# A decoder layer on one core: the sum of gated branches kept in DRAM by accumulating DMAs, its SBUF room given to a sixth weight slot and two high-part buffers

## Chip, cores and metric

One core of a Trainium2 chip runs the kernel. The metric is the device time of one execution in microseconds (us); a shorter one is better.

## The reference, cut

The kernel computes one layer for 256 tokens of width 2048: a norm, one wide input product, four attention branches, their gated sum and an output product. All numbers are float32.

```python
h = rms_norm(x, norm_w)
p = h @ w_in                                  # (256, 2048) @ (2048, 17492)
(z, gate, dsa_qkv, idx_q, idx_k, idx_w, fox_qkv, fox_f, diff_qkv, dil_qkv) = jnp.split(p, IN_OFFSETS, axis=-1)
# o_dsa: top-64 of indexer scores, then attention; o_fox: forgetting; o_diff: difference of two
# softmax maps; o_dil: dilated windows.  Four heads of 128 each.
for b in range(4):
    y = branches[b].reshape(bsz, seq, 512) * jax.nn.silu(z_parts[b])
    term = jax.nn.sigmoid(g_parts[b]) * (y @ w_branch[b])      # (256, 2048)
    merged = term if merged is None else merged + term
x = x + merged @ w_out
return rms_norm(x, final_norm_w)
```

## The kernel before

**Tiles and units.** The weights are read once, in blocks of 512 rows by 512 columns (1 MB). A *unit* (`Unit`) is one use of one such block. Its matmuls run in float32r, so each block is split: ScalarE copies it rounded, the *high part* (`whi`, L192), and VectorE subtracts that from the block, the *low part* (`wlo`, L193), each in two halves of 1024 columns. `three` (L342) then issues three matmuls for one product: high by high (L345), high weight by low activation (L346), low weight by high activation (L347).

**Slots and buffers.** A block is loaded by SP's queue into one of five *slots* (`raw0` to `raw4`, 8 KB of a partition each). `free` issues the next load of a slot when the split of its block is done (L195 to L198); the load itself waits until every reader of the old block is done. High and low parts have six buffers each (`HALVES`). In the main loop (L1148) the half that is split stands five halves ahead of the half whose matmuls are issued (L1153), so each engine's queue holds splits, evictions and attention steps in one fixed order.

**Seven products.** `seven` (L415) computes a 256 by 1024 block of a product in 11 units. For half of the rows of the weights it uses seven products instead of eight of a two by two scheme: the weight blocks B11, B12, B21, B22 stand in slots 0, 1, 3, 2 and are added in place on VectorE (`plus`, L171) between uses, and the activations' combinations are in `sf` (`act_forms`). The other half is done plainly by c2a, c2b, c1a and c1b, 24 matmuls each, all four in slot 4 (L448). The order is P5 P1 P3 c2a P6 c2b P7 P2 c1a P4 c1b. What a unit wants done first (`pre`, in-place sums) is issued two units ahead, right after the split of a unit's second half (L1141).

**Order of the program.** Indexer units; then for each of four branches a seven-product for q and k, one for z and v, two for the gates (`gate_units`), and four projections of 24 matmuls (`branch_units`). Attention steps are generators (`active`) that `run_threads` advances by one step for each 20 matmuls or more; a unit's `need` runs the named ones to their end first. The gate tiles g (four buffers, shared with q, k, z) hold sigmoids. After a projection VectorE multiplies it by g (L904) and adds it to m (L905), a 16 KB tile of a partition. In the last branch `merge_thread` transposes m into mT, and `act_forms` makes sf from its first half; then comes the product with w_out, one seven-product and two blocks of plain units. `open_final` loads x and the final norm's weights again (L918, L920) on POOL's queue, 3 MB.

Of the kernel before, what the change touches and what calls it, by code (L numbers as in the profile page):

```python
# [31 lines left out]
HALVES = 6  # L32
PACE = 20
SLOTS = 5
# [46 lines left out]
class Unit:  # L81
# [3 lines left out]

    def __init__(self, raw, mm, post=(), need=(), start=(), pre=(), frees=None, loads=None):
        self.raw, self.k0, self.nk, self.n = raw, raw.k0, raw.nk, raw.n
        self.mm, self.post = mm, list(post)
        self.need, self.start, self.pre = list(need), list(start), list(pre)
        self.after = []  # L90
        self.frees = [raw] if frees is None else list(frees)
        self.loads = [raw] if loads is None else list(loads)
        self.parts = [None, None]
        self.cost = 24
# [7 lines left out]
    def part(self, k, i):  # L102
        half = self.nk // 2
        return self.parts[k // half][i][:, k % half * self.n:(k % half + 1) * self.n]
# [3 lines left out]
def body(ctx: ExitStack, tc, x, norm_w, w_in, fox_b_f, lq1, lk1, lq2, lk2, subln_w,  # L108
# [70 lines left out]
    def split(u, h, hi=None, lo=None, parts=1, part=None):  # L179

        n_ = u.nk // 2 * u.n
        if not part:
            if hi is None:
                hi = wp.tile([P, 1024], F32R, name="whi", tag="whi", bufs=HALVES)
                lo = wp.tile([P, 1024], F32R, name="wlo", tag="wlo", bufs=HALVES)
            u.parts[h] = (hi[:, :n_], lo[:, :n_])
        hi, lo = u.parts[h]
        raw = u.raw.tile[:, h * n_:(h + 1) * n_]
        step = n_ // parts
        for i in range(parts) if part is None else (part,):  # L190
            s_ = slice(i * step, (i + 1) * step)
            nc.scalar.activation(hi[:, s_], raw[:, s_], AF.Copy)  # L192
            nc.vector.tensor_tensor(lo[:, s_], raw[:, s_], hi[:, s_].bitcast(F32),  # L193
                                    op=ALU.subtract)
        if h == 1:  # L195
            for f in u.after:
                f()
            free(u.frees)  # L198

# [34 lines left out]
    xs = big.tile([P, 2, D], F32, name="xs", tag="m")  # L234
# [162 lines left out]
    def act_forms(T, pool, tag):  # L397

        V["sf"] = big.tile([P, 2, 8, 2, P], F32R, name="sf", tag="sf")
        a = pool.tile([P, 2, 8, P], F32, name="asum", tag=tag)  # L400
        for t in range(2):
            c = T[:, 0:8, :, t * P:(t + 1) * P].bitcast(F32)
            nc.vector.tensor_tensor(a[:, t], c[:, :, 0], c[:, :, 1], op=ALU.add)
        yield
        a11, a12, a21, a22 = a[:, 0, 0:4], a[:, 0, 4:8], a[:, 1, 0:4], a[:, 1, 4:8]
# [4 lines left out]
        for t in range(2):  # L410
            nc.scalar.activation(V["sf"][:, t, :, 0], a[:, t], AF.Copy)
            nc.vector.tensor_tensor(V["sf"][:, t, :, 1], a[:, t],
                                    V["sf"][:, t, :, 0].bitcast(F32), op=ALU.subtract)

    def seven(src, c1, c2, base, ev, name, need=((), (), (), ()), start=()):  # L415

        st = {}
        B11, B12 = Raw(0, src, 0, 4, c1, 512), Raw(1, src, 0, 4, c2, 512)
        B21, B22 = Raw(3, src, 4, 4, c1, 512), Raw(2, src, 4, 4, c2, 512)

        def whole(half, k0):
            t = slice(half * P, (half + 1) * P)
            return lambda k: (base()[:, k0 + k, 0, t], base()[:, k0 + k, 1, t])

# [3 lines left out]
        def product(bank, act, first=False):  # L428
            def mm(u, h):
                if first and h == 0:  # L430
                    st[bank] = main_ps(name)
# [25 lines left out]
        u5 = Unit(B12, product("W", form(1, 4), True), loads=[B12, B11, B22, B21], frees=[],  # L457
                  post=[read(ev.p5, "W")], need=need[0])
        u1 = Unit(B11, product("Y", whole(0, 0), True), loads=[], frees=[],
                  post=[read(ev.p1, "Y")])  # L460
        u3 = Unit(B22, product("Z", form(0, 4), True), loads=[], frees=[])
        c2a = c(8, c2, "ZW")
        c2a.need += need[1]
        u6 = Unit(B12, product("Y", form(0, 0)), loads=[], frees=[], post=[read(ev.u2, "Y")])
        c2b = c(12, c2, "ZW")
        c2b.need += need[2]
        c2b.post += [read(ev.c12, "Z", True)]
        u7 = Unit(B11, product("Y", form(1, 0)), loads=[], post=[read(ev.u3, "Y")])
        u2 = Unit(B21, product("X", whole(0, 4), True), loads=[], frees=[],
                  post=[read(ev.c22, "W", True)])  # L470
        c1a = c(8, c1, "XY")
        u4 = Unit(B21, product("Y", whole(1, 4)), loads=[])
        u4.pre += [lambda: plus(B21, B12), lambda: free([B12])]
        c1b = c(12, c1, "XY")
        c1b.post += [read(ev.c11, "X", True), read(ev.c21, "Y", True), ev.end]
        c1b.start += start
        c1b.need += need[3]
        u5.pre += [lambda: plus(B12, B11)]
        u6.pre += [lambda: plus(B12, B22), lambda: free([B22])]
        u7.pre += [lambda: plus(B11, B12, ALU.subtract)]  # L480
        for u in (u1, u5, u3, u6, u7, u2, u4):
            u.cost = 12
        return [u5, u1, u3, c2a, u6, c2b, u7, u2, c1a, u4, c1b]

    class Tok:


        def __init__(self, dst, s1, s2, end):
            self.dst, self.s1, self.s2, self.end = dst, s1, s2, end
# [51 lines left out]
    def qkvz_units(b, off, scale, start):  # L541


        def two(names):
            if b == 0:
                if "tok" not in V:
                    V["tok"] = big.tile([P, 4, 2, 512], F32, name="tok", tag="m")
                return V["tok"][:, names == "zv"], V["tok"][:, 2 + (names == "zv")]
            return [big.tile([P, 2, 512], F32, name="tok", tag="g", bufs=4) for _ in range(2)]

        def dst_qk():
            V["q_"], V["k_"] = d = two("qk")
            return d
# [636 lines left out]
```

## Time and profile before

| | |
|---|---|
| median of two runs | 1085.38 us (1085.06 to 1085.7) |
| profiled execution, its own time | 1085.43 us |
| its span, first to last instruction | 1083.7 us |
| TensorE matmuls busy | 979.7 us (90%), 4443 |
| VectorE busy | 867.1 us (80%), 1035 instructions |
| ScalarE busy | 622.9 us (57%) |
| granted TensorE clock, mean | 0.969 of full speed |
| DMA | 187.42 MB, mean 173 GB/s |

The profile is one execution. Busy time is that of each engine's own instructions; matmuls overlap, so their durations are longer than their distance. "Idle before" is the time an engine stood still ahead of an instruction, and what follows the arrow is the instruction or transfer that ended it. The chain of waits follows the last instruction back through what released each step.

### The profile page before, as it was taken

The page shows a single profiled execution, that of the slowest core. Times are in us where ns is not written, and L with a number is a line of the kernel's source. Part 1 is how long each engine was busy: PE and PEld are TensorE (multiplying, and loading weights), DVE is VectorE, ACT ScalarE, POOL GpSimd, SP SyncE. Part 2 cuts the span into 40 slices and gives each one's busy share as a digit, 9 for nine tenths or more (in the row PEclk, how much of TensorE's full clock was granted, in tenths as well). Part 3 has the DMA queues.
Part 4 walks back from the last instruction along what each step waited for, and adds up shares of the span by engine and source line. Part 5 has one row for each costly group of instructions (what it writes and reads, how often), then busy time and mean ns, then how long its engine had stood idle before and what let it go on. Part 6 is the DMA issues. An engine that isn't in the chain of part 4 may idle for free.

```text
span 1083.7 us, 12059 instructions
## 1 busy us (share of the span) xinstructions
PE 979.7 (90%) x4443; PEld 793.9 (73%) x4443; DVE 867.1 (80%) x1035; ACT 622.9 (57%) x809; POOL 31.7 (3%) x51
## 2 busy tenths in 40 slices
PE   9989996888999999899899997869999979876997
PEld 8867884676788787777788775658888858654886
DVE  5799989778689988777899876869988968588663
ACT  5665764676546565855465657554465676534551
POOL 2010000000000000000000000000000000000010
PEclk9989997999999999999999999989999999987999
DMA  9836451535646465365266451562646534742542
GB/s 322 254 101 201 151 195 53 180 117 194 217 153 228 161 224 167 121 229 191 97 233 219 169 191 42 184 207 95 233 155 232 176 136 156 268 158 78 195 155 78
DMA packets 97739, 187.42 MB, mean 173 GB/s; under 512 B 7555, under 2 KB 9765, under 8 KB 97296
## 3 DMA queue, kind: packets, MB, share of 16 engines
q1 hardware_dynamic: 96240, 181.06, 49.1%
q0 software_dynamic: 1408, 5.59, 1.5%
q8 instruction: 35, 0.57, 0.2%
q14 instruction: 24, 0.20, 0.1%
q10 hardware_dynamic: 32, 0.01, 0.0%
HBM read 184.52 MB, written 2.12 MB: 172 GB/s over the span
## 4 chain that ended last, share of the span: by engine, by line
PE 55%; DVE 21%; DMA 8%; issue 8%; ACT 8%; POOL 0%; ACTq 0%; DVEq 0%; POOLq 0%
DVE wlo L193 12%; DMA raw<-in_w_in_dram 5%; PE ps_qk L347 5%; PE ps_qk L345 5%; PE ps_qk L346 5%; PE ps_zv L347 4%; ACT whi L192 4%; PE ps_zv L345 4%; PE ps_zv L346 4%; PE ps_g L345 4%; PE ps_g L346 4%; PE ps_g L347 4%; PE ps_o L346 2%; PE ps_o L347 2%; PE ps_iq L350 2%
## 5 line engine op out<-in xcount | busy, mean ns | idle before, releaser
L193 DVE TENSOR_TENSOR wlo<-raw,whi 128x1024 fp32r<-128x1024 f32 (+1 forms) x439 | 518.6, 1221 | 160.5 <-ACT whi L192 155.0
L192 ACT ACTIVATE whi<-raw 128x1024 fp32r<-128x1024 f32 (+1 forms) x439 | 441.4, 1048 | 295.7 <-DMA raw<-in_w_in_dram 121.3
L171 DVE TENSOR_TENSOR raw<-raw 128x2048 f32<-128x2048 f32 x68 | 155.5, 2287 | 7.6 <-DMA raw<-in_w_out_dram 3.8
L347 PE MATMUL ps_g<-wlo,hT 128*128 128x512 f32 x352 | 140.7, 400 | 19.5 <-DVE wlo L193 19.5
L345 PE MATMUL ps_g<-whi,hT 128*128 128x512 f32 x352 | 141.8, 403 | 12.0 <-ACT g L504 10.4
L346 PE MATMUL ps_g<-whi,hT 128*128 128x512 f32 x352 | 139.0, 395 | 0.0
L347 PEld LDWEIGHTS ps_g<-wlo,hT 128*128 128x128 f32 x352 | 67.3, 191 | 39.2 <-DVE wlo L193 25.0
L345 PEld LDWEIGHTS ps_g<-whi,hT 128*128 128x128 f32 x352 | 67.2, 191 | 30.2 <-ACT g L504 13.9
L346 PEld LDWEIGHTS ps_g<-whi,hT 128*128 128x128 f32 x352 | 67.1, 191 | 13.6
L347 PE MATMUL ps_qk<-wlo,hT 128*128 128x512 f32 x176 | 69.0, 392 | 2.3 <-DVE wlo L193 2.3
L345 PE MATMUL ps_qk<-whi,hT 128*128 128x512 f32 x176 | 68.8, 391 | 1.7 <-ACT whi L192 1.0
L347 PE MATMUL ps_zv<-wlo,hT 128*128 128x512 f32 x176 | 69.2, 393 | 1.0 <-DVE wlo L193 0.9
L345 PE MATMUL ps_zv<-whi,hT 128*128 128x512 f32 x176 | 68.9, 392 | 0.0
L346 PE MATMUL ps_qk<-whi,hT 128*128 128x512 f32 x176 | 68.6, 390 | 0.0
L346 PE MATMUL ps_zv<-whi,hT 128*128 128x512 f32 x176 | 68.5, 389 | 0.0
L345 PE MATMUL ps_b<-whi,yT 128*128 128x512 f32 x128 | 52.5, 410 | 11.1 <-DVE g L904 7.0
L345 PE MATMUL ps_g<-whi,sf 128*128 128x512 f32 x128 | 54.2, 424 | 6.3 <-DVE g L500 4.0
L347 PE MATMUL ps_g<-wlo,sf 128*128 128x512 f32 x128 | 50.8, 397 | 1.6 <-DVE wlo L193 1.6
L346 PE MATMUL ps_b<-whi,yT 128*128 128x512 f32 x128 | 51.5, 403 | 0.0
L347 PE MATMUL ps_b<-wlo,yT 128*128 128x512 f32 x128 | 51.4, 401 | 0.0
L346 PE MATMUL ps_g<-whi,sf 128*128 128x512 f32 x128 | 50.4, 394 | 0.0
L346 PE MATMUL ps_o<-whi,mT 128*128 128x512 f32 (+1 forms) x112 | 41.2, 368 | 0.9 <-DVE mT L890 0.9
(264 smaller groups left out, 1526.7 us busy)
## 6 DMA issues: line engine op xcount, KB each, us to landing
raw<-in_w_in_dram SPq DMA_DIRECT2D x132, 1024.0 KB, 5.2
raw<-in_w_branch_dram SPq DMA_DIRECT2D x16, 1024.0 KB, 5.2
raw<-in_w_out_dram SPq DMA_DIRECT2D x16, 1024.0 KB, 5.2
raw<-in_w_in_dram SPq DMA_DIRECT2D x7, 512.0 KB, 9.6
xs<-in_x_dram SPq DMA_DIRECT2D x8, 256.0 KB, 7.7
xf<-in_x_dram POOLq DMA_DIRECT2D x2, 1024.0 KB, 8.6
bias<-vdr POOLq DMA_DIRECT2D x3, 512.0 KB, 4.1
out_dram<-xf SPq DMA_DIRECT2D x5, 256.0 KB, 2.7
```

What stands on the lines that cost most here:

```text
L171: nc.vector.tensor_tensor(to.tile, of.tile, to.tile, op=op)
L192: nc.scalar.activation(hi[:, s_], raw[:, s_], AF.Copy)
L193: nc.vector.tensor_tensor(lo[:, s_], raw[:, s_], hi[:, s_].bitcast(F32), op=ALU.subtract)
L345: nc.tensor.matmul(ps, ahi, u.hi(k)[:, cols], start=first, stop=False, skip_group_check=on)
L346: nc.tensor.matmul(ps, alo, u.hi(k)[:, cols], start=False, stop=False, skip_group_check=on)
L347: nc.tensor.matmul(ps, ahi, u.lo(k)[:, cols], start=False, stop=last, skip_group_check=on)
L350: nc.tensor.matmul(ps[:m], u.hi(k)[:, j * P:j * P + m], hT[:, k0 + k].rearrange("p a s -> p (a s)"), start=k0 + k == 0, stop=False)
```

## The change

The tile m goes. For the first three branches the gating product is written by POOL's queue to four DRAM tiles (`md`), the first branch plainly and the next two with an accumulating DMA. In the last branch `load_m` reads them back and one VectorE addition of 1024 columns for each joins them to the last gated projection. `xs`, q and k of the first branch, z of the first branch and the kept parts at the end, which had lain in m's room, move to the rooms of `sf`, `y` and `g`.

m's 16 KB are given to a sixth slot (8 KB) and to two more high-part buffers. Plain blocks alternate between slots 4 and 5. High parts are issued seven halves ahead, low parts five halves ahead as before; `pre` follows the high part of a second half, so it now stands ahead of two low halves that it stood behind. P4's in-place sum moves to P2's `after`, which is the same place among the low parts. In the product with w_out (`late`) the first rows are done plainly and the last by seven products, in the order c2a c2b P1 P5 P3 P2 P6 P7 c1a P4 c1b, and sf is made from the second half of mT. x and the final norm's weights are loaded after the first projection of the last branch is evicted, behind two `load_m`.

```diff
-HALVES = 6
+HI = 8
+LO = 6
-SLOTS = 5
+SLOTS = 6
...
-    def split(u, h, hi=None, lo=None, parts=1, part=None):
+    def split_hi(u, h, kept=None, parts=1, part=None):
...
+                u.parts[0][h] = wp.tile([P, 1024], F32R, name="whi", tag="whi", bufs=HI)[:, :n_]
...
+            nc.scalar.activation(u.parts[0][h][:, s_], raw[:, s_], AF.Copy)
+    def split_lo(u, h, kept=None, parts=1, part=None):
...
+                u.parts[1][h] = wp.tile([P, 1024], F32R, name="wlo", tag="wlo", bufs=LO)[:, :n_]
...
+            nc.vector.tensor_tensor(u.parts[1][h][:, s_], raw[:, s_],
+                                    u.parts[0][h][:, s_].bitcast(F32), op=ALU.subtract)
         if h == 1:
             for f in u.after:
                 f()
             free(u.frees)
...
-    xs = big.tile([P, 2, D], F32, name="xs", tag="m")
+    xs = big.tile([P, 2, D], F32, name="xs", tag="sf")
...
-    def act_forms(T, pool, tag):
+    def act_forms(T, k0, room):
...
+            c = T[:, k0:k0 + 8, :, t * P:(t + 1) * P].bitcast(F32)
...
+        s0, p0 = (8, 0) if late else (0, 8)
+        B11, B12 = Raw(0, src, s0, 4, c1, 512), Raw(1, src, s0, 4, c2, 512)
+        B21, B22 = Raw(3, src, s0 + 4, 4, c1, 512), Raw(2, src, s0 + 4, 4, c2, 512)
...
-            return Unit(Raw(4, src, k0, 4, c0, 512), plain(k0, two))
+            return Unit(Raw(4 + k0 // 4 % 2, src, k0, 4, c0, 512), plain(k0, two))
...
-        u4.pre += [lambda: plus(B21, B12), lambda: free([B12])]
+        u2.after += [lambda: plus(B21, B12)] + ([] if late else [lambda: free([B12])])
...
+        if late:
+            u6.after += [lambda: free([B12])]
+            u7.post += [read(ev.c12, "Z", True), read(ev.c22, "W", True)]
+            return [c2a, c2b, u1, u5, u3, u2, u6, u7, c1a, u4, c1b]
...
+        def tok():
+            return big.tile([P, 2, 512], F32, name="tok", tag="g", bufs=4)
...
+                both = big.tile([P, 2, 2, 512], F32, name="tok2", tag="y")
...
+    md = [dram.tile([P, 1024], F32, name=f"md{n}") for n in range(4)]
+    def load_m(n):
+        V["m"][n] = V["mg"].tile([P, 1024], F32, name="mp", tag="mp", bufs=2)
+        nc.gpsimd.dma_start(V["m"][n], md[n])
...
     def merge_thread(n):
-        if n != 1:
-            yield
...
-        m = V["m"]
+        g = V["g"][n]
+        gf = g.rearrange("p t c -> p (t c)")
+        nc.vector.tensor_tensor(gf, gf, V["m"][n], op=ALU.add)
+        if n < 2:
+            load_m(n + 2)
+        yield
...
-        if n == 1:
-            yield from act_forms(mT, V["mg"], "asum")
+        if n == 3:
+            yield
+            yield from act_forms(mT, 8, lambda: [
+                big.tile([P, 8, P], F32, name="asum", tag="g", bufs=4) for _ in range(2)])
     def branch_units(b, n):
         def ev(ps):
-            if b == 0 and n == 0:
-                V["m"] = big.tile([P, 4, 2, 512], F32, name="m", tag="m")
-            m, g = V["m"], V["g"][n]
+            g = V["g"][n]
             for t in range(2):
-                if b == 0:
-                    nc.vector.tensor_tensor(m[:, n, t], ps[t], g[:, t], op=ALU.mult)
-                else:
-                    nc.vector.tensor_tensor(g[:, t], ps[t], g[:, t], op=ALU.mult)
-                    nc.vector.tensor_tensor(m[:, n, t], m[:, n, t], g[:, t], op=ALU.add)
+                nc.vector.tensor_tensor(g[:, t], ps[t], g[:, t], op=ALU.mult)
+            if b < 3:
+                nc.gpsimd.dma_start(md[n], g.rearrange("p t c -> p (t c)"),
+                                    accum_op=ALU.add if b else ALU.bypass)
+            elif n == 0:
+                for i in range(2):
+                    load_m(i)
...
-                         (0, 2, 4, 3)[n:n + 1], ev,
+                         (0, 2, 4, 5)[n:n + 1], ev,
...
+    units[last_gate + 1].post.append(load_final)
+    units += seven(w_out, 0, 512, lambda: V["mT"], Out(), "ps_o", late=True,
+                   need={"c2a": ["merge0", "merge1"], "P1": ["merge2"], "P5": ["merge3"]})
+    units += out_units(2, (4, 5, 0, 2))
+    units += out_units(3, (1, 3, 4, 5))
...
     load(waiting[4].popleft())
+    load(waiting[5].popleft())
...
+    def high(q):
         i, h = divmod(q, 2)
...
+        if i < len(units):
+            split_hi(units[i], h, kept(units[i]))
         if h and i + 2 < len(units):
             for f in units[i + 2].pre:
                 f()
+    def low(q):
+        i, h = divmod(q, 2)
+        if i < len(units):
+            split_lo(units[i], h, kept(units[i]))
...
         for h in range(2):
-            half(2 * i + h + HALVES - 1)
+            low(2 * i + h + LO - 1)
+            high(2 * i + h + HI - 1)
             u.mm(u, h)
```

## Rows read from the trace of the kernel before

**Rows 1.** The page, part 1: busy us, share of the span, instructions

```profile
PE 979.7 (90%) x4443; PEld 793.9 (73%) x4443; DVE 867.1 (80%) x1035; ACT 622.9 (57%) x809; POOL 31.7 (3%) x51
```

**Rows 2.** Stages: length, PE, PEld, DVE, ACT, POOL busy us, clock, DMA share, GB/s

```profile
166.60:236.40 69.80, 51.92 (x216) 40.97 (x214) 57.65 (x112) 38.55 (x53) 0.00 (x0) 0.88 0.38 132
...
350.80:394.50 43.70, 43.38 (x198) 35.22 (x197) 39.69 (x35) 25.88 (x30) 0.00 (x0) 1.00 0.59 208
394.50:447.80 53.30, 48.10 (x216) 39.14 (x214) 42.15 (x55) 37.82 (x52) 0.00 (x0) 0.97 0.47 159
...
495.30:519.50 24.20, 22.30 (x97) 17.83 (x96) 20.39 (x23) 10.69 (x12) 0.00 (x0) 1.00 0.59 207
...
661.40:730.30 68.90, 50.27 (x225) 38.03 (x224) 49.65 (x77) 41.94 (x74) 5.62 (x9) 0.95 0.45 154
...
938.90:984.00 45.10, 26.84 (x114) 21.27 (x112) 34.55 (x41) 14.72 (x19) 1.34 (x3) 0.84 0.47 181
984.00:1031.70 47.70, 46.17 (x197) 36.94 (x198) 37.67 (x35) 24.80 (x30) 2.60 (x2) 0.94 0.49 163
```

**Rows 3.** TensorE's waits: what for; us in total, times, longest us

```profile
PE ps_g L347 <- DVE wlo L193: 21.1, 14, 10.4
PE ps_o L345 <- ACT sf L411: 11.3, 1, 11.3
PE ps_g L345 <- ACT g L504: 10.4, 7, 2.5
PE ptp L764 <- DVE lg L773: 10.0, 3, 4.5
PE otd L858 <- DVE on L851: 8.4, 1, 8.4
PE ps_b L345 <- DVE g L904: 7.0, 2, 5.4
...
PE ps_g L345 <- ACT whi L192: 3.9, 3, 2.4
```

**Rows 4.** Waits of VectorE and ScalarE in the same view

```profile
DVE wlo L193 <- ACT whi L192: 155.0, 92, 4.3
...
ACT whi L192 <- DMA raw<-in_w_in_dram: 121.3, 36, 6.9
```

**Rows 5.** Chain of waits around 428: start us, us, what

```profile
428.88 5.07 DMA raw<-in_w_in_dram
434.05 1.07 ACT whi L192
```

**Rows 6.** Order of time, TensorE, second branch's gates: start us, us, what

```profile
431.06 0.63 PE L345 MATMUL ps_g<-whi,hT 128*128 128x512 f32 x1
...
431.49 0.63 PE L346 MATMUL ps_g<-whi,hT 128*128 128x512 f32 x1
...
434.32 0.40 PE L345 MATMUL ps_g<-whi,hT 128*128 128x512 f32 x1
...
434.55 0.39 PE L346 MATMUL ps_g<-whi,hT 128*128 128x512 f32 x1
```

**Rows 7.** VectorE's groups by line: busy us, mean ns, idle us before

```profile
L193 DVE TENSOR_TENSOR wlo<-raw,whi 128x1024 fp32r<-128x1024 f32 (+1 forms) x439 | 518.6, 1221 | 160.5 <-ACT whi L192 155.0 <-PE o L810 2.7 <-PE ps_qk L347 1.7
L171 DVE TENSOR_TENSOR raw<-raw 128x2048 f32<-128x2048 f32 x68 | 155.5, 2287 | 7.6 <-DMA raw<-in_w_out_dram 3.8 <-DMA raw<-in_w_in_dram 2.9 <-issue 0.3
L905 DVE TENSOR_TENSOR m<-m,g 128x512 f32<-128x512 f32 x24 | 16.6, 692 | 0.8
```

**Rows 8.** The page, part 6: DMA issues, KB each, median us to landing

```profile
bias<-vdr POOLq DMA_DIRECT2D x3, 512.0 KB, 4.1
```

**Rows 9.** Chain of waits, last merge: start us, us, what

```profile
939.09 14.01 DMA raw<-in_w_out_dram
```

**Rows 10.** Start of the span by stages, columns as in rows 2

```profile
0.00:27.10 27.10, 25.99 (x151) 23.57 (x152) 15.06 (x24) 14.34 (x25) 5.98 (x17) 1.00 0.95 322
```

**Rows 11.** Order of time on VectorE, last merge

```profile
953.11 2.29 DVE L171 TENSOR_TENSOR raw<-raw 128x2048 f32<-128x2048 f32 x1 [3.75 <-DMA raw<-in_w_out_dram]
```

More of the change, by code (lines that the diff above doesn't have):

```diff
@@ L103, in part @@
         half = self.nk // 2
-        return self.parts[k // half][i][:, k % half * self.n:(k % half + 1) * self.n]
+        return self.parts[i][k // half][:, k % half * self.n:(k % half + 1) * self.n]
 @with_exitstack
@@ L198, in split @@
             free(u.frees)
+    def split(u, h, parts=1, part=None):
+        split_hi(u, h, None, parts, part)
+        split_lo(u, h, None, parts, part)
     nw = const.tile([16, P], F32, name="nw")
@@ L455, in read @@
             return g
[L457 to L464, printed above, removed]
@@ L475, in seven, with unit @@
[L475 to L482, printed above, removed]
+        def unit(what, raw, mm, post=(), frees=(), loads=(), pre=()):
+            u = Unit(raw, mm, frees=frees, loads=loads, post=post, pre=pre, need=need.get(what, ()))
+            u.cost = 12
+            return u
@@ new lines, in seven @@
+        u5 = unit("P5", B12, product("V" if late else "W", form(1, 4), True),
+                  [read(ev.p5, "V" if late else "W")], loads=[B12, B11, B22, B21],
+                  pre=[lambda: plus(B12, B11)])
+        u1 = unit("P1", B11, product("Y", whole(0, s0), True), [read(ev.p1, "Y")])
+        u3 = unit("P3", B22, product("Z", form(0, 4), not late))
+        u6 = unit("P6", B12, product("Y", form(0, 0)), [read(ev.u2, "Y")],
+                  pre=[lambda: plus(B12, B22), lambda: free([B22])])
@@ new lines, in seven @@
+        u7 = unit("P7", B11, product("Y", form(1, 0)), [read(ev.u3, "Y")], frees=[B11],
+                  pre=[lambda: plus(B11, B12, ALU.subtract)])
+        u2 = unit("P2", B21, product("X", whole(0, s0 + 4), True))
+        u2.after += [lambda: plus(B21, B12)] + ([] if late else [lambda: free([B12])])
+        u4 = unit("P4", B21, product("Y", whole(1, s0 + 4)), frees=[B21])
+        c2a, c2b = c(p0, c2, "ZW"), c(p0 + 4, c2, "ZW")
+        c1a, c1b = c(p0, c1, "XY"), c(p0 + 4, c1, "XY")
+        c2a.need += need.get("c2a", ())
@@ L980, in p5 @@
             self.add(ps, 0, 1)
+            self.add(ps, 1, 1)
         def u2(self, ps):
@@ L998, in c21 @@
             out_col(ps, 1, 0, 512, 0)
-        def end(self):
-            pass
     def out_units(n, slots):
@@ L1143, in half @@
                 f()
-    for q in range(2 * RAMP + 1, 2 * RAMP + HALVES - 1):
-        half(q)
+    def low(q):
+        i, h = divmod(q, 2)
+        if i < len(units):
+            split_lo(units[i], h, kept(units[i]))
+    for q in range(2 * RAMP + 1, 2 * RAMP + HI - 1):
+        high(q)
+        if q < 2 * RAMP + LO - 1:
+            low(q)
     since = 0
```

130 lines of the change are left out of this document (60 added, 70 removed).

## The prediction, made before the change was run

> **What bounds the kernel now.** I read the busy shares first, then the busy times by stage, then who TensorE waits for, and last two stretches of the trace.
>
> TensorE is busy for 90% of the span and VectorE for 80% [rows 1]. This is an in-order pipeline of two nearly full engines, and the most that better feeding can give is TensorE's 104 us of idle time (1083.7 - 979.7) plus what a slow clock costs after it. The stages [rows 2] show where that is. From 350.8 to 394.5 (query-key-value product of the second branch) TensorE is idle for 0.3 us of 43.7: deeper buffers give nothing there. In the first gate product of the same branch (394.5 to 447.8) 5.2 us are idle, in that of the first branch 17.9, in the third branch's second gate product 18.6, and in the last merge 18.3 (45.1 - 26.84). So the gain must come from the gate stages, where attention shares ScalarE and VectorE with the splitting, and from the end.
>
> What TensorE waits for there [rows 3]: low parts 21.1 us, low-product operands at the end (sf) 11.3, ScalarE's eviction L504 10.4, a scaled softmax 10.0, the last step of differential attention 8.4, VectorE's gating product L904 7.0, high parts 3.9. Behind the first of these stand two others [rows 4]: VectorE waits 155.0 us, 92 times, for ScalarE's high part, and ScalarE 121.3 us for a weight load. The stretch at 428.88 shows why [rows 5]: the four plain blocks of a seven-product all live in slot 4, so the load goes out only when the block before has been split to its end, lands 5.07 us later, and high and low part follow. Meanwhile TensorE runs dry, and its clock falls: around 431 two matmuls are 0.43 us apart, three us later 0.23 [rows 6]. That is the lower of its two levels (1.2 GHz against 2.4), so part of an idle time is paid twice.
>
> **The change part by part.** The sum is made against the profiled execution, 1085.43 us (span 1083.7 and 1.7 around it); the median shown is 1085.38.
>
> *Sixth slot, eight high buffers, highs two halves ahead.* Plain blocks alternate between slots 4 and 5, so a load goes out one plain block (24 matmuls) and some 12-matmul products earlier: over 60 matmuls at 0.23 us, 13.8 us, lie between, against 5.07 for the load. High parts stand in ScalarE's queue ahead of the exponentials and sigmoids they now follow. TensorE's waits for low parts of the gates are 21.1; 10.4 of that is one wait behind the top-k rounds on VectorE, which stay where they are. This leaves 10.7, and 3.9 for highs: 14.6, bounds 5 and 14.6, taken 13. Smaller rows of the same kind elsewhere (products of q, k, z) add 3.
> One step behind the same delay are the scaled softmax (10.0: VectorE scaled late because it stood behind a late low part), taken 8, bounds 0 and 10; and L504 (10.4: ScalarE did sigmoid, exponentials and two highs in a row without an idle moment, so only its start moves), taken 3, bounds 0 and 10. The 8.4 of differential attention is a chain of its own steps, forced before the projection: nothing.
>
> *The sum in DRAM.* VectorE loses 24 adds of 0.69 us (16.6) and gains four of 1024 columns, about 1.22 each by the row of the low part of that size: 11.7 us less work [rows 7]. In the projection stages TensorE is nearly full (22.30 of 24.2 [rows 2]), so this gives little: taken 3, bounds 0 and 6. New are 12 writes of 512 KB from POOL's queue, eight accumulating, and four reads. No row shows an accumulating write. From below, a plain 512 KB transfer lands in 4.1 us [rows 8]; from above, the slowest transfer of the trace took 14.01 [rows 9]. The gate buffer that it holds is next written (as key) after two projections and one product, 60 matmuls, 13.8 us: hidden but for the last 0.2. What it takes from weight loads: at the 322 GB/s of the start [rows 10] 512 KB is 1.6 us of the 16 DMA engines; these are 59% busy in a projection stage [rows 2], which leaves (1 - 0.59) x 24.2 / 4 = 2.5 us for each write. It hides; taken 1 us in all for collisions, bounds 0 and 12 x (14.0 - 2.5) = 138, a far end that I weigh as a rival.
> The Trainium skill (Collectives: The Full Stack, The bandwidth ceiling: the fold count and why AG ≠ RS ≠ AR) says that an add in a DMA needs two source reads and so runs at about half of a copy's rate. No row here shows it; by it a write takes 3.2 us of the engines instead of 1.6, and eight of them would cost 8 x 0.7, about 6 us, more, which makes the sum 1049, an estimate from that page.
>
> *In-place sums move.* The sum for the next seven-product's first block now stands two low parts earlier in VectorE's queue. Its weights are loaded only after the previous product's last use of slot 1: in-place sum 2.29, load 5.07 [rows 5, 7]. Before, four lows (4.9 us) ran in between, now two (2.4). So VectorE may idle up to 2.5 us at each of 16 transitions, and behind it stand two lows, then evictions, and on ScalarE the first highs of the next product. Where TensorE has all it wants, the lows are early and this costs nothing; in the start-up one low stands behind such a sum (1.2). Taken 3, bounds 0 and 40.
>
> *The end.* Before, the load of a w_out block goes out at 939.09 beside three loads from POOL and takes 14.01; VectorE stands at the in-place sum until 953.11 with the gating products behind it [rows 9, 11], and TensorE waits 5.4 of the 7.0 for L904. After, the first blocks are plain and the in-place sum is three units later; POOL brings 1 MB more. I take 2 to 3 us of stall in the four projections instead of 12: projections 96 matmuls (21.8), transposes 1, stall 2.5, so they end at 938.9 + 25.3 = 964.2 rather than 972.7, where the 11.3 wait begins (984.0 - 11.3): 8.5 gained, slow clock in it.
> Then the count from the last projection to the sf operands, in VectorE's order: 13 operations of 512 columns (two gating products, six low halves of mT, one eviction, four form sums) at 0.69, ten of 1024 (six lows, two merges, two form sums) at 1.22, two in-place sums at 2.29: 9.0 + 12.2 + 4.6, and two copies on ScalarE of about 1 us, 28 us. TensorE covers 13.6 of it with the three units now put ahead (60 matmuls), waits for the rest, and has 120 matmuls left, 27.2, and 2 for the clock: 57. Before it was 11.3 + 47.7 = 59 [rows 2, 3]. The new order gives only 2. Together 10.5, bounds 2 and 19.
>
> *Clock.* In the gate and merge stages the granted clock is 0.97 to 0.84 [rows 2]; (1 - clock) x length is 8.4, 1.6, 3.4, 7.2 and 2.9, 23.5, an upper bound since some of that time is idle anyway and the top-k and sf waits stay. Outside the end, taken 6.
>
> **Sum:** 13 + 3 + 8 + 3 + 3 + 10.5 + 6 = 46.5, less 1 and 3: 42.5. 1085.4 - 42.5 = 1043. With the high end of each term (14.6, 3, 10, 10, 6, 19 and 10 for the clock) it would be 1013; with half the waits for parts (8), half the softmax wait (4), the 8.5 of the projections, 2 for the clock and the losses of 4, it would be 1067.
>
> **The rivals.**
> *The waits only move.* ScalarE meets the highs earlier in its queue, waits there for loads or in-place sums, and exponentials and evictions behind it come late. For it: rows 4 show ScalarE already waiting for loads, and rows 3 hold waits on attention itself. Against it: the loads go out earlier too. Then half of the waits for parts (8), the end (10.5), 3 of the branch adds, less 4: 1068.
> *VectorE without lead.* In gate stages it has 42.15 of 53.3 [rows 2], and if every low that comes early is followed by an in-place sum that waits, 16 transitions take 1.5 each: 24 in place of the 3 taken, 1064.
> *Accumulating writes hold the weight loads (the other side).* Place: three projection stages and what follows. A write that takes w us of the engines costs 12 x (w - 2.5). The gain is eaten at 42.5 / 12 + 2.5 = 6.0 us, and slower by 2% (21.7 us) is reached at 7.9. At 9 us it gives 1043 + 78 = 1121. For it: nothing but that no row shows such a write and that a transfer beside others took 14.01. Against it: 4.1 for a whole plain one. The skill's half rate, 3.2, stays far below.
>
> **How the numbers follow.** Both waits go as summed: 0.72. Waits move: 0.13. VectorE without lead: 0.09. Writes hold the loads: 0.06. About 2% can be told from no change, that is 1063.7 to 1107.1. The first case lies under 1063.7 but for 0.05; of the second a sixth and of the third nearly half (together 0.06) lie under it too; the fourth is two thirds slower. Faster 0.67 + 0.06 + 0.01 = 0.74, same 0.22, slower 0.04. The predicted time is 1043. The range goes from 1016 to 1071: at the low end almost all waits but the 10.4, 8.4 and the sf wait gone, at the high end both rivals within 2% up to a little past their centres; about 0.1 is left on either side.
>
> **What would show it.** Right: the slot-4 loads follow each other without the 5 us pieces in the chain; VectorE's wait for highs falls from 155.0 below 70; TensorE's idle time falls by some 35; the softmax wait almost goes, L504 stays; the second branch's first gate product takes about 48 us instead of 53.3; the sf wait stays at 10 or so. Wrong: ScalarE's wait for loads or in-place sums grows; low parts wait behind in-place sums at each transition; an accumulating write lands later than 13.8 us and a copy on ScalarE waits for it; stages that were full, like 350.8 to 394.5, become longer.

## The result, and the profile after

The changed kernel takes 1009.98 us (median of 2 runs, 1009.36 to 1010.6) against 1085.38: a ratio of 0.9305, 95% interval 0.9265 to 0.9345. The forecast was 1043, range 1016 to 1071. The direction was right; the gain, 75.4 us, is 33 more than forecast, and the time lies outside the range. The profiled execution took 1009.36 us, with a span of 1007.7.

Part 1 of the page of the changed kernel: busy us, share of the span, instructions.

```profile
PE 958.3 (95%) x4443; PEld 793.4 (79%) x4443; DVE 856.1 (85%) x1016; ACT 630.1 (63%) x809; POOL 47.5 (5%) x67
```

Against [rows 1], TensorE's idle time fell from 104.0 to 49.4 us, that is by 54.6, and its busy time for the same 4443 matmuls by 21.4; the two make the whole of the span's 76.0. So more than a quarter of the gain is in busy time. Part of it is the clock: (1 - granted clock) x span, an upper bound, falls from 33.6 (0.969) to 23.2 us (0.977), by about 10. The other 11 I put down to short waits inside busy time: a matmul's record in the last two of [rows 6] is 0.40 us long and the next one starts after 0.23, so a pause shorter than the difference counts as busy. That is argued from these rows, not measured.

The stages of the changed kernel, columns as in [rows 2], in the order of those rows: the first branch's first gate product, the second branch's last product ahead of its gates, its first gate product, its four projections, the third branch's second gate product, the last projections and merges, and the seven-product of w_out.

```profile
163.80:224.50 60.70, 50.26 (x215) 40.48 (x214) 58.32 (x107) 39.18 (x53) 0.00 (x0) 0.89 0.42 139
...
330.70:373.40 42.70, 42.70 (x197) 35.36 (x196) 38.28 (x34) 26.82 (x30) 0.00 (x0) 1.00 0.58 197
373.40:419.10 45.70, 45.70 (x216) 38.14 (x214) 43.38 (x56) 38.65 (x52) 0.00 (x0) 1.00 0.55 184
...
462.70:484.50 21.80, 21.80 (x98) 18.06 (x97) 18.26 (x19) 9.43 (x11) 2.64 (x3) 1.00 0.73 176
...
617.00:670.20 53.20, 47.47 (x225) 38.81 (x224) 44.27 (x72) 35.14 (x65) 5.33 (x8) 0.97 0.59 198
...
866.60:896.30 29.70, 26.39 (x112) 21.71 (x111) 18.52 (x19) 10.08 (x13) 1.06 (x2) 0.89 0.71 267
896.30:955.60 59.30, 46.07 (x199) 37.12 (x198) 51.37 (x51) 28.24 (x34) 3.95 (x2) 0.88 0.42 149
```

The second branch's first gate product went from 53.3 to 45.7 us, with not a moment of idle TensorE and the full clock: no better feeding could shorten it. Six of the eight gate stages now stand there. The last line of the same view, taken over the eight gate stages alone, of the kernel before and then of the changed one:

```profile
sum 444.10, PE 383.37 PEld 303.22 DVE 342.76 ACT 282.76 POOL 6.70; mean PE 47.92 PEld 37.90 DVE 42.84 ACT 35.35 POOL 0.84
```

```profile
sum 385.10, PE 368.93 PEld 302.80 DVE 345.29 ACT 287.72 POOL 7.98; mean PE 46.12 PEld 37.85 DVE 43.16 ACT 35.96 POOL 1.00
```

The gates give 59.0 of the 76 us: 44.6 of idle time and 14.4 of busy time. The end gives little: last projections and seven-product together went from 92.8 [rows 2] to 89.0. The rest is 5.2 in the other projections and 9.4 in the products of q, k, z and v, less 1.4 elsewhere.

The waits of the changed kernel (us in total, times, longest):

```profile
PE ps_o L362 <- ACT sf L428: 11.7, 1, 11.7
PE ps_g L364 <- DVE wlo L206: 8.3, 1, 8.3
PE otd L880 <- DVE on L873: 5.7, 1, 5.7
...
PE mtp L916 <- DVE g L908: 3.3, 1, 3.3
...
PE ps_g L362 <- ACT g L530: 1.4, 1, 1.4
...
ACT whi L193 <- DVE raw L173: 93.3, 27, 13.4
...
DVE raw L173 <- DMA raw<-in_w_in_dram: 30.2, 15, 4.0
...
DVE wlo L206 <- ACT whi L193: 19.1, 16, 8.7
```

Against [rows 3, 4]: low parts 21.1 to 8.3 (the one wait behind the top-k rounds), the gate eviction (L504 before, L530 now) 10.4 to 1.4, the scaled softmax from 10.0 to nothing on the list, VectorE's wait for highs 155.0 to 19.1, ScalarE's wait for a weight load of w_in from 121.3 to 0.5. In their place ScalarE waits 93.3 us for in-place sums, where it was 53.6 before; no wait of TensorE for a high part of the gates is left.

### The profile page after: what moved, and what is told of

It reads as the page before. It is cut to its first block, busy times and chain, and to the rows that moved or that the text cites. A ratio compares the mean times of both kernels' runs of the same rounds, so it can differ in the third digit from the quotient of the medians.

```text
span 1007.7 us, 12090 instructions
## 1 busy us (share of the span) xinstructions
PE 958.3 (95%) x4443; PEld 793.4 (79%) x4443; DVE 856.1 (85%) x1016; ACT 630.1 (63%) x809; POOL 47.5 (5%) x67
## 4 chain that ended last, share of the span: by engine, by line
PE 81%; DVE 10%; issue 3%; ACT 3%; DMA 2%; POOL 0%; ACTq 0%; POOLq 0%; DVEq 0%
PE ps_g L362 10%; PE ps_g L363 10%; PE ps_g L364 10%; PE ps_zv L362 5%; PE ps_zv L364 5%; PE ps_zv L363 5%; PE ps_qk L364 5%; PE ps_qk L362 5%; PE ps_qk L363 5%; DVE wlo L206 4%; PE ps_o L363 2%; PE ps_b L362 2%; PE ps_b L363 2%; PE ps_b L364 2%; PE ps_o L362 2%
## 5 line engine op out<-in xcount | busy, mean ns | idle before, releaser
L193 ACT ACTIVATE whi<-raw 128x1024 fp32r<-128x1024 f32 (+1 forms) x439 | 444.6, 1051 | 231.2 <-DVE raw L173 93.3
L206 DVE TENSOR_TENSOR wlo<-raw,whi 128x1024 fp32r<-128x1024 f32 (+1 forms) x439 | 519.0, 1218 | 52.5 <-ACT whi L193 19.1
L173 DVE TENSOR_TENSOR raw<-raw 128x2048 f32<-128x2048 f32 x68 | 155.6, 2288 | 30.8 <-DMA raw<-in_w_in_dram 30.2
L364 PE MATMUL ps_g<-wlo,hT 128*128 128x512 f32 x352 | 137.7, 391 | 8.3 <-DVE wlo L206 8.3
L362 PE MATMUL ps_g<-whi,hT 128*128 128x512 f32 x352 | 138.9, 395 | 1.4 <-ACT g L530 1.4
L363 PE MATMUL ps_g<-whi,hT 128*128 128x512 f32 x352 | 137.3, 390 | 0.0
```

Source lines behind the costliest of these rows:

```text
L173: nc.vector.tensor_tensor(to.tile, of.tile, to.tile, op=op)
L193: nc.scalar.activation(u.parts[0][h][:, s_], raw[:, s_], AF.Copy)
L206: nc.vector.tensor_tensor(u.parts[1][h][:, s_], raw[:, s_], u.parts[0][h][:, s_].bitcast(F32), op=ALU.subtract)
L362: nc.tensor.matmul(ps, ahi, u.hi(k)[:, cols], start=first, stop=False, skip_group_check=on)
L363: nc.tensor.matmul(ps, alo, u.hi(k)[:, cols], start=False, stop=False, skip_group_check=on)
L364: nc.tensor.matmul(ps, ahi, u.lo(k)[:, cols], start=False, stop=last, skip_group_check=on)
```

## The experiments

All kernels here but the first are variants of the changed one. The ratios are against the kernel before on the same chip, whose median there stands beside them.

| kernel | median us | before us | ratio, 95% interval |
|---|---|---|---|
| changed kernel again | 1009.4 | 1083.2 | 0.9326 (0.9312 to 0.9340) |
| five slots | 1119.5 | 1084.6 | 1.0328 (1.0310 to 1.0345) |
| highs level with lows | 1054.8 | 1084.6 | 0.9725 (0.9711 to 0.9740) |
| both undone | 1087.7 | 1084.6 | 1.0027 (1.0015 to 1.0039) |
| seven level | 1060.7 | 1083.2 | 0.9796 (0.9782 to 0.9811) |
| in-place sums later | 1019.6 | 1084.6 | 0.9403 (0.9389 to 0.9417) |
| adds put back | 1013.7 | 1080.8 | 0.9385 (0.9369 to 0.9401) |
| plain writes | 1009.9 | 1080.8 | 0.9348 (0.9333 to 0.9364) |
| old order at the end | 1014.8 | 1080.8 | 0.9391 (0.9377 to 0.9405) |
| final loads later | 1003.0 | 1080.8 | 0.9287 (0.9273 to 0.9302) |
| plain column first | 999.2 | 1083.2 | 0.9230 (0.9215 to 0.9245) |
| column first, loads later | 1000.0 | 1083.2 | 0.9233 (0.9219 to 0.9247) |

**The changed kernel again**, with no edit, for comparison.

> The changed kernel itself, on the chip of the next three: 1006 to 1011, so that what its variants gain is read beside it.

Measured 1009.4.

**Five slots.**

```
-            return Unit(Raw(4 + k0 // 4 % 2, src, ...
+            return Unit(Raw(4 + k0 // 4 % 2 * late, src, ...
-                         (0, 2, 4, 5)[n:n + 1], ev,
+                         (0, 2, 4, 5 if b == 3 else 3)[n:n + 1], ev,
```

> The changed kernel, with all plain blocks of the seven-products back in slot 4 (the sixth slot is left to the last branch and w_out, so the end is as in the changed kernel). High parts keep eight buffers and stand two halves ahead. Theory 'slot': the gates ran dry because a plain block's load went out only after the block before it had been split to its end; then most of the 58.8 us that the eight gate stages gained is given back and the time is 1050 or more, with ScalarE waiting over 100 us for weight loads again. Theory 'queue order': the highs stood behind exponentials, sigmoids and evictions; then most stays, 1015 to 1025. Theory 'each alone is worth little': the load and the queue delay stand in one chain and both have to go, so this is near the kernel with both undone, 1055 to 1070.

**Highs level with their lows.** Six high buffers; the in-place sums (`pre`) move from `high` to the end of `low`.

```
-HI = 8
+HI = 6
-            low(2 * i + h + LO - 1)
             high(2 * i + h + HI - 1)
+            low(2 * i + h + LO - 1)
```

> The changed kernel with six high buffers and each high part issued just ahead of its low part, as before the change (in-place sums behind the low part again, too); the sixth slot stays. Theory 'slot': most of the gain stays, 1015 to 1025, and VectorE's wait for highs goes from 19 us to some 40. Theory 'queue order': most of the gates' gain is lost, 1050 or more, and VectorE's wait for highs is above 100 us. Theory 'each alone is worth little': 1055 to 1070, like the kernel with both undone.

**Both undone**, the two edits together.

> Both edits of the pipeline undone: plain blocks in slot 4 (but for the end), six high buffers, highs level with the lows. What stays of the change is the sum in DRAM, without VectorE's 24 adds, and the new order at the end. By the recorded terms (3 for the adds, 10.5 for the end, 1 of clock) 1085.4 - 14.5 = 1071; by the stage lengths of the changed kernel (end 3.7, projections 5.4) 1076. Were VectorE's work itself what starved the gates, it would stay below 1050.

Measured 1119.5, 1054.8 and 1087.7. No theory had all three. With both undone nothing is left of the gain, where the recorded terms had 1071 and the stage lengths 1076: the DRAM sum and the new order at the end bring nothing without the pipeline edits. The sixth slot alone is worth 33 us (1087.7 - 1054.8), and 110 where the highs are ahead (1119.5 - 1009.4). The highs two halves ahead cost 32 us with five slots (1119.5 - 1087.7). The earlier place of the in-place sums goes with them here; the two are told apart only with six slots, below. So "each alone is worth little" is wrong too: one edit is good alone, the other is bad alone. Waits with five slots:

```profile
ACT whi L193 <- DMA raw<-in_w_in_dram: 218.6, 46, 10.8
...
PE ps_g L362 <- ACT g L530: 37.0, 8, 5.9
...
DVE wlo L206 <- ACT whi L193: 70.2, 43, 7.4
...
PE ps_qk L362 <- ACT tok L530: 18.6, 4, 6.4
```

ScalarE runs into the load of slot 4 two halves earlier and stands at it for 218.6 us, and the evictions queued behind that high hold a PSUM bank that TensorE needs (37.0 and 18.6). VectorE's wait for highs falls to 70.2, from 173.6 with both undone, and the time is longer all the same. This is the recorded rival "the waits only move", to the letter; it is the sixth slot that keeps it from happening. With the slot, and the highs level:

```profile
DVE wlo L206 <- ACT whi L193: 138.5, 97, 12.3
...
ACT g L554 <- DVE g L534: 45.5, 8, 6.4
...
PE ps_g L364 <- DVE wlo L206: 13.5, 10, 7.4
...
PE ps_g L362 <- ACT g L530: 10.4, 7, 2.5
```

No wait of a high for a load of w_in is left, and yet VectorE still waits 138.5 us for highs, and TensorE as long for the eviction as before the change (10.4, seven times). What is left is no load of w_in but the order between ScalarE and VectorE.

**Seven level** buffers of each part: the same room as eight and six, the splitting one half further ahead, but again each high just ahead of its low, and the in-place sums behind the low.

```
-HI = 8
-LO = 6
+HI = 7
+LO = 7
...
```

> The changed kernel with seven high and seven low buffers (the same room as eight and six) and each high level with its low, in-place sums behind the low: the splitting is one half further ahead of TensorE than in the kernel with six level ones, but VectorE still follows ScalarE directly. Theory 'ring': what cost the gates their time is that VectorE stands in its queue for a high, ScalarE's sigmoid stands for the eviction behind that low, and the exponentials and highs behind the sigmoid make the next high late; then one half more of depth does little: 1045 to 1055, VectorE's wait for highs stays above 100 us and ScalarE's sigmoid still waits some 45 us for L534. Theory 'depth': what counts is how early the parts are for TensorE; then this stands halfway between six level (1054.8) and eight ahead with late sums (1019.6) or better: 1020 to 1037.

Measured 1060.7, no better than six level. "Depth" falls. The time of "ring", 1045 to 1055, is missed too, by 6 us on the slow side; what it said of the waits came out:

```profile
DVE wlo L206 <- ACT whi L193: 147.3, 100, 9.9
ACT g L554 <- DVE g L534: 40.7, 8, 5.9
...
PE ps_g L362 <- DVE g L526: 17.9, 6, 5.8
...
PE ps_g L362 <- DVE tok L544: 8.8, 1, 8.8
```

The low parts are early now; they are no longer among TensorE's large waits. Instead it waits for evictions on VectorE (L526, L544). In one such place VectorE stands 2.01 us for a high, works from 452.83 without a pause, and comes to L526 only at 462.97, behind lows and an in-place sum; TensorE stands 3.71 us for it.

That ring can be read off the kernel before, around the place of [rows 6]. ScalarE in order of time, then VectorE, then TensorE (start us, us, what, idle time before it and what ended it):

```profile
406.06 1.04 ACT L192 ACTIVATE whi<-raw 128x1024 fp32r<-128x1024 f32 x1
...
417.99 1.06 ACT L192 ACTIVATE whi<-raw 128x1024 fp32r<-128x1024 f32 x1 [3.06 <-DMA raw<-in_w_in_dram]
...
422.85 0.63 ACT L528 ACTIVATE g<-g 128x512 f32<-128x512 f32 x1 [2.50 <-DVE g L508]
...
426.55 1.99 ACT L192 ACTIVATE whi<-raw 128x1024 fp32r<-128x1024 f32 x2
428.44 0.67 ACT L504 ACTIVATE g<-ps_g,rst 128x512 f32<-128x512 f32 x1
```

```profile
407.13 1.23 DVE L193 TENSOR_TENSOR wlo<-raw,whi 128x1024 fp32r<-128x1024 f32 x1 [2.00 <-ACT whi L192]
...
418.72 2.29 DVE L171 TENSOR_TENSOR raw<-raw 128x2048 f32<-128x2048 f32 x1
420.93 1.22 DVE L193 TENSOR_TENSOR wlo<-raw,whi 128x1024 fp32r<-128x1024 f32 x1
422.07 0.75 DVE L508 SCALAR_TENSOR_TENSOR g<-ps_g,rst,g 128x512 f32<-128x512 f32 x1
...
427.62 3.69 DVE L193 TENSOR_TENSOR wlo<-raw,whi 128x1024 fp32r<-128x1024 f32 x3 [4.06 <-ACT whi L192]
...
435.14 1.23 DVE L193 TENSOR_TENSOR wlo<-raw,whi 128x1024 fp32r<-128x1024 f32 x1 [1.63 <-ACT whi L192]
```

```profile
429.16 0.50 PE L345 MATMUL ps_g<-whi,hT 128*128 128x512 f32 x1 [2.47 <-ACT g L504]
...
437.90 0.30 PE L764 MATMUL ptp<-ident,lg 128*128 128x128 f32 x1 [2.72 <-DVE lg L773]
```

VectorE stands 2.00 us for a high that ScalarE does behind exponentials (406.06). From that low at 407.13 to 423.6 it works without a pause, so the eviction L508 comes only at 422.07, behind lows and two in-place sums. The sigmoid that reads it has by then waited 2.50 us (422.85); the exponentials and the two highs behind it follow (426.55), and for these VectorE has meanwhile stood idle for 4.06 us. The path is back at VectorE's wait for a high: a ring. The eviction L504 comes last on ScalarE, at 428.44, and TensorE stands 2.47 us for it.

A load can be a link of this ring. The one ahead of 417.99 is not: its high was done at 419.05, and the low at 420.93 stood behind an in-place sum, with no idle time of its own. The next one is: it goes out at 428.88 [rows 5], once the first of the lows from 427.62 is done, its own low waits 1.63 us for the high (435.14), and the softmax that VectorE scales behind that low keeps TensorE 2.72 us. The sixth slot cuts the ring at such loads. The lead of the highs cuts it where VectorE waits: the highs behind the exponentials are then those of halves further on, and VectorE does not stand for them.

What the ring costs is seen on VectorE better than on TensorE. Its wait for highs in the second branch's first gate product, before and in the changed kernel:

```profile
DVE wlo L193 <- ACT whi L192: 10.8, 5, 4.1
```

```profile
DVE wlo L206 <- ACT whi L193: 0.2, 1, 0.2
```

Before, VectorE's work of 42.15 us [rows 2] and this wait make 53.0 of the 53.3 us of the stage: VectorE set its pace, while TensorE's own list has just 2.5 and 2.7 us of waits there. Six slots with level highs have no load in the ring, still wait 10.8 in this stage, and take 51.5. In the changed kernel VectorE has 43.4 us of work and TensorE's 45.7 set the length. VectorE need not set the pace: with five slots and the highs ahead its wait is 0.4 and the stage still takes 52.9, there with ScalarE standing for loads.

In the changed kernel the same sigmoid (L554) and eviction (L530) go like this:

```profile
395.40 1.06 ACT L193 ACTIVATE whi<-raw 128x1024 fp32r<-128x1024 f32 x1 [3.90 <-DVE raw L173]
...
397.78 0.63 ACT L554 ACTIVATE g<-g 128x512 f32<-128x512 f32 x1
...
403.38 0.67 ACT L530 ACTIVATE g<-ps_g,rst 128x512 f32<-128x512 f32 x1
```

No idle time stands ahead of this sigmoid; ScalarE waits one step earlier, 3.90 us for an in-place sum. From the sigmoid to the eviction 5.60 us pass, as before (5.59), but the whole row of work starts in time for TensorE, which is never idle in this stage and waits 1.4 us for that eviction in the whole run.

**In-place sums later.** `pre` moves from `high` to the end of `low`, nothing else.

> The changed kernel with each in-place sum of a seven-product issued behind the low part of its half, as before the change, instead of behind the high part two halves earlier; nothing else. By the recorded step the earlier place costs 3 us (VectorE idles 30 us ahead of such sums for loads): then this kernel takes 1006 to 1008. If the place costs nothing because the lows are early: 1009 to 1010. If it is a gain, since the next product's first highs can start earlier: 1012 to 1020.

Measured 1019.6, so the earlier place gains about 10 us (8 by the ratios), where 3 lost were forecast. The waits of this kernel:

```profile
ACT whi L193 <- DVE raw L173: 166.5, 54, 17.0
...
PE ps_g L364 <- DVE wlo L206: 12.7, 3, 8.9
...
PE ps_g L362 <- ACT g L530: 4.2, 4, 1.5
```

VectorE no longer idles 30.2 us for loads ahead of these sums (4.3 are left), but ScalarE, whose next highs need them, stands 166.5 us for them instead of 93.3, with evictions behind. The idle time on VectorE that I feared is real, and here it costs less than the highs gain.

**Adds put back.** A maximum of each gate half with itself behind the gating product:

```
+                if b:
+                    nc.vector.tensor_tensor(g[:, t], g[:, t], g[:, t], op=ALU.max)
```

> The changed kernel with VectorE's 24 operations of 512 columns put back behind the gating products of branches 1 to 3, as a maximum of each gate half with itself, which leaves the value as it is: 24 x 0.69 = 16.6 us more work for VectorE, in the place where the adds of m stood. By the recorded term (fewer branch adds, 3, bounds 0 and 6) 1013, between 1010 and 1016. If the adds lay in the shadow of a full TensorE, as the kernel with both pipeline edits undone says (no faster than before): 1010. If VectorE, now busy for 85%, has become the bound: up to 1026.

Measured 1013.7, 4 more by the medians (6 by the ratios across two chips, 3.0 by the profiled spans). The projections of the second and third branch take 21.8 and 23.5 us as without the adds; the last projections go from 29.7 to 31.8 and the seven-product from 59.3 to 60.7. The term of 3 has its size, but at the end, where the stages grow by 2.1 and 1.4 us, and not in the projections ahead.

**Plain writes.**

```
-                                    accum_op=ALU.add if b else ALU.bypass)
+                                    accum_op=ALU.bypass)
```

> The changed kernel with the eight accumulating writes made plain ones (the DRAM sum then holds the third branch alone, so the first two are left out of the result): same sizes, places and queue. If the accumulation is hidden, as recorded: 1009 to 1011, and each write's time from issue to landing tells its price (5.3 us when accumulating; 4.1 for a plain transfer of that size). If it takes DMA time away from the weight loads: faster by up to 6 us, 1004.

Measured 1009.9, no faster than the changed kernel (1009.4; 2 us slower by the ratios): the accumulation costs no time that can be seen here. The writes from issue to landing, of the changed kernel and then of this one:

```profile
md<-g POOLq DMA_DIRECT2D x12, 512.0 KB, 5.3
```

```profile
md<-g POOLq DMA_DIRECT2D x12, 512.0 KB, 3.0
```

**The old order at the end**: `late=False` for w_out, form sums from the first half of the merged columns, merges 0 and 1 needed by P5.

> The changed kernel with the seven-product of w_out in its old order: form sums from the first half of the merged columns, P5, P1, P3 first, merges 0 and 1 needed ahead of P5, 2 and 3 ahead of the two plain blocks. By the recorded count the new order is worth 2 us: 1012. If the end's small gain (92.8 to 89.1 us for last merge and seven-product) is all that the new order and the pipeline brought together, the old order may be as good: 1008 to 1011. If the new order hides the form sums better than counted: 1015 to 1022.

Measured 1014.8, so the new order is worth 5 us (7 by the ratios). The two end stages take 92.8 us (46.3 and 46.5) against 89.0.

**Final loads later.**

```
-    units[last_gate + 1].post.append(load_final)
             load_m(n + 2)
+        if n == 1:
+            load_final()
```

> The changed kernel with the 3 MB of x and the final weights asked for in the merge of the second column block, behind that merge's own read of the sum, instead of behind the last branch's first projection. Theory 'shared DMA': the w_out loads that go out at 862 to 874 land after 16.2, 13.5 and 10 us because these 3 MB run beside them; ScalarE (13.2) and VectorE (8.7) wait for them and the gating product behind keeps TensorE 3.3 us; then these loads land in some 6 us, the last merge's stage goes from 29.8 to 25, and the time to 1004 to 1006. Rival 'VectorE sets the end': the form sums are set by VectorE's own work from the last projection on, so nothing is gained: 1009 to 1011. Rival 'moved too far': x lands after the first eviction needs it, 1012 or more.

Measured 1003.0, 6.9 less than the kernel with plain writes on the same chip (4 by the ratios against the changed kernel): "shared DMA" holds. The loads that go out between 860 and 890, median us to landing, changed kernel and then this one:

```profile
raw<-in_w_out_dram SPq DMA_DIRECT2D x5, 1024.0 KB, 13.5
```

```profile
raw<-in_w_out_dram SPq DMA_DIRECT2D x5, 1024.0 KB, 5.6
```

The last projections then take 23.5 us instead of 29.7, with no idle time, and the seven-product 59.0; TensorE's wait for sf stays at 11.7.

**Plain column first.** The third column block of w_out, which needs no form sums, ahead of the seven-product:

```
...
+            active.append(("oforms", act_forms(mT, 8, ...)))
...
+    o2 = out_units(2, (1, 3, 0, 2))
+    for n in range(4):
+        o2[n].need.append(f"merge{n}")
+    units += o2
     units += seven(w_out, ..., late=True, need={"P5": ["oforms"]})
-    units += out_units(2, (4, 5, 0, 2))
-    units += out_units(3, (1, 3, 4, 5))
+    units += out_units(3, (2, 1, 0, 4))
```

> The changed kernel with the plain third column block of w_out (4 units, 96 matmuls, 21.8 us) put ahead of the seven-product, each unit needing just one merge, and the form sums in a thread of their own that P5 needs. Count from rows of the changed kernel: from the last projection to the form operands VectorE has 28 us, plus 8 lows at 1.22 and two evictions at 0.69, some 39; TensorE now has 156 matmuls, 35.3 us, ahead of P5, so of the 11.7 us of waiting about 4 stay: 1002 (1000 to 1004). Rival: VectorE sets the end and its work is the same, the wait is only spread over the four units: 1007 to 1011.

Measured 999.2, 10.3 less than the changed kernel on the same chip. Its four end stages (projections, plain column, seven-product, last column):

```profile
866.40:889.90 23.50, 23.50 (x114) 19.60 (x113) 18.21 (x20) 10.45 (x13) 1.06 (x2) 1.00 0.95 363
889.90:913.50 23.60, 23.60 (x115) 19.75 (x113) 19.95 (x21) 11.27 (x14) 0.00 (x0) 1.00 0.53 179
913.50:967.20 53.70, 46.51 (x182) 36.16 (x182) 46.66 (x41) 26.98 (x33) 7.45 (x4) 0.90 0.27 98
967.20:997.40 30.20, 22.50 (x145) 20.43 (x143) 11.15 (x19) 5.78 (x14) 5.30 (x5) 0.96 0.19 70
```

The seven-product loses 5.6 us (59.3 to 53.7), and the projections 6.2 (29.7 to 23.5); the plain column takes 23.6 where it took 21.8. So the forecast of 1002 had the wait for sf and not the stall in the projections. The loads go out at the same moments as in the changed kernel and those beside the final loads land as late; but the first two blocks are now in slots 1 and 3, whose loads went out at 845.9 and 853.2 and landed by 859.2, and the late ones are needed two units later. The wait for sf is gone; 7 us of others stay in the seven-product, for evictions and lows on VectorE (4.3 and 2.7), which is busy for 46.7 of 53.7.

**Column first and loads later.**

> The plain third column block ahead of the seven-product and the 3 MB of final loads later, together. The first takes the wait for the form operands, the second the late w_out loads (1003.0 alone, against 1010 for the changed kernel). If both add up: 994 to 997. If the first finds the wait already covered or the later x is now missed by the evictions: 1001 to 1004.

Measured 1000.0: they do not add up. Each alone takes the same stall out of the last projections, which run from first to last matmul in 22.4 us in all three kernels and 28.8 in the changed one, and later loads alone gave little else. The plain column first alone takes the same time within the spread (998.9 to 1000.7 against 998.6 to 1001.1) with one edit less.

## Why the prediction was wrong

**What was right.** TensorE ran dry in the gates; the slot-4 load is a link of the chain; the top-k and sf waits stay (8.3 and 11.7); the softmax wait goes; VectorE's wait for highs falls below 70; the accumulating writes hide. One sign of being wrong came true, ScalarE's wait for in-place sums (53.6 to 93.3), and did no harm. The sum's parts missed as follows.

**Eviction L504, taken 3: 9.0.** The step that failed is the sentence that ScalarE "did sigmoid, exponentials and two highs in a row without an idle moment, so only its start moves". One instruction further back it had waited 2.50 us for L508, and L508 stood in VectorE's queue behind lows that had stood for highs. The sum priced TensorE's waits as separate rows, each with a share that might stay, where they were links of one ring that VectorE's waits for highs kept slow; those were read, 155.0 us, and given no price. Cut, the ring gives nearly all of them: low and high parts 16.7 (12.8 and 3.9) where 13 were taken, the softmax 10.0 where 8 were, differential attention 2.7 where nothing was.

The stretch at 428.88 was misread in the same way. The load there does not make TensorE run dry before 437.90; the idle time just ahead of the lower clock is the 2.47 us for L504, at 429.16.

**Clock, taken 6: about 10.** Busy time fell by 21.4 us, 14.4 of it in the gates, but the granted clock accounts for about 10 (33.6 to 23.2). The rest, which I put down to short waits inside busy time, had no term in the sum: two gate stages went from 45.23 to 43.60 and from 45.16 to 43.60 at a clock of 1.00 before and after. The bound of 23.5 was one of five stages, not of the span. The gates now run at a clock of 1.00 but for the two with waits left (0.89 and 0.97). At the end the clock stays at 0.89 and 0.88.

**In-place sums, taken 3 lost: 8 to 10 gained.** I priced VectorE's idle time and named ScalarE's highs behind it, but gave no credit for these highs coming earlier. The sign was wrong, not only the size.

**Fewer branch adds, taken 3 in the projections.** The projections of the first three branches did gain about 5 us, but not by this: with both pipeline edits undone they still take 24.2, 24.0 and 24.1 us. The adds are worth 3 to 6, at the end. That the size is the one taken is luck.

**The end, taken 10.5: 3.8.** "2 to 3 us of stall in the four projections" was the wrong size: the stage takes 29.7 us against 21.8 of projections, 1 of transposes and the 2.5, because w_out loads share the DMA engines with the final loads (13.5 us to landing against 5.6). I had the 14.01 of [rows 9] for just this and did not carry it over. The 28 us from the last projection to the form operands came out as counted: the projections end at 895.7, and P5 starts at 923.7, after the 11.7 of waiting. The new order is worth 5 to 7, not 2.

**Collisions, taken 1: none seen.** The eight accumulating writes landed after 5.1 to 5.9 us, far from the 13.8 at which a copy would wait.

By the runs the chain of edits is: DRAM sum and new order 3 us lost (1084.6 to 1087.7), sixth slot 33 gained, highs ahead with late sums 35 (1054.8 to 1019.6), sums earlier 10. The forecast gave the middle two and the clock about 33 together, and the first 12.5. Separate worths do not exist here: the highs ahead, with the sums earlier, are a loss of 32 without the slot.

The range was too narrow for the same reasons: even the high ends of all terms together gave 1013. The move of the sums had no bound on the side of a gain, and the busy time beyond the clock had no term at all.

## What to carry to other kernels

When two in-order engines feed each other, look for a ring: go back from a late eviction past the instructions that run without a pause to the one that waited, and ask what that one's releaser stood behind; if the path returns to the first engine, price the ring as a whole, by the work and the waits of the engine that sets the pace, and not TensorE's waits row by row. Here a cut gave nearly all of them. Moving work ahead in an in-order queue pays only if its input is there, or the wait moves with it (32 us lost with five slots, 45 gained with six, the in-place sums moved along both times), so price the pair and not the parts. At the end of a kernel, put work that needs nothing late ahead of work that does, and keep loads that are needed later off the DMA engines while the next weights come.

## What the runs showed of the hardware

An accumulating write of 512 KB to DRAM took 5.1 to 5.9 us to land, a plain one at the same places 2.9 to 4.8 (medians 5.3 and 3.0 of the twelve, four of them plain in both). The software queue took 5.3% of the 16 engines' span with accumulation and 3.8% without: 15 us over eight writes, 1.9 each. The Trainium skill (Collectives: The Full Stack, The bandwidth ceiling: the fold count and why AG ≠ RS ≠ AR) has the reduce step of a collective, whose add needs two source reads, run at about half of a copy's rate. The prediction carried that over to these writes, which are no collective: 1.6 us more by my estimate. The trace, with 1.9, agrees with it in size, and the plain writes show no effect on the time.

One step more of depth made things slower: seven level buffers took 1060.7 us where six took 1054.8. The waits say that evictions stood behind more lows; that this is all of the 6 us is argued, not shown. I did not try other leads than none and two halves.
